# Sigmoids computed from tanh of half the argument in a two-layer hybrid trunk on one core

## The chip, the core and the metric

The kernel runs on one core of one Trainium2 chip. The metric is the device time of one execution in microseconds (us). Three runs of the kernel before took 2874.05, 2875.11 and 2875.87 us; the median is 2875.11 us.

## What is computed

The reference is one step of a trunk of two layers. The same weights serve 128 context tokens and 512 latent tokens, so 640 tokens run through everything. Each layer is a feed-forward sublayer, a mixer and another feed-forward sublayer, each with a layer norm. The mixer of the even layer joins windowed attention with a bidirectional mLSTM, that of the odd layer joins attention with a bidirectional HGRN2. Sigmoids stand in both mixers, and silu(x) is x * sigmoid(x):

```python
# even mixer, behind the two mLSTM scans
yb = sigmoid(bo) * rms(hf + flip(hb), norm_g)
# odd mixer
q = silu(cq)
def hgrn_gates(fp):
    f = lbh + (1.0 - lbh) * sigmoid(fp)
    return log(f), 1.0 - f
...
yc = rms(of + flip(ob), norm_g) * silu(cg)
```

The even mixer also needs log_sigmoid of its gates (computed with Abs, Exp and Ln), both need Exp for the softmax of the attention, and the feed-forward sublayers use silu.

## The kernel before, in words

All activations lie transposed, features on the 128 partitions and the 640 tokens along the free dimension, in two halves of 384 and 256 tokens (`HALVES`), or in five chunks of 128. Products with weights are done three times on split halves of the operands (`mm3`, `proj_pair`), so the weights are loaded with a DMA (`unit`), rounded on ACT and subtracted on DVE (`split`).

The mixers `even` and `odd` are written as Python generators, which `weave` runs in turn: one step of the attention, one step of the projections of the heads, and later steps of the mLSTM or HGRN2 heads. So instructions of the projections stand between those of the attention. The code is not the order on the engines: each engine runs a queue in order, and a planner sets these queues from the dependencies, the order of the code and its own view of the times.

The steps that matter here:

- `att_probs`: for one chunk of 128 queries and four heads, PE writes the scores into a bank (tile `s`), DVE takes the maximum, ACT takes Exp with a bias column and a sum (tiles `pq`, `E`, `bm`), DVE takes the reciprocal of the sum (`su`) and scales. `att_out` transposes the result on PE (`pT`), splits it on ACT and DVE (`pr`) and multiplies with the values (`pv`).
- `mlstm_in` (L1014), four heads: two projections with `proj_steps`, then `proj_pair` with five chunks. Of each chunk ACT copies the values (tile `va` or part of `mi`) and takes Sigmoid of the output gate `so`.
- `hgrn_cols` and `hgrn_in` (L1245, L1262), four heads: the projections for the query (Sigmoid, then a product on DVE) and for the two forget gates (Sigmoid, then multiply and add with the lower bound on DVE), each in two halves; then `proj_pair` with five chunks, of which ACT copies the values and takes Sigmoid of the gate, which DVE multiplies.
- `head_out` (L775): sum of squares on ACT, the power -1/2 on POOL (`hrs`), the product with the gate on DVE (`yn`), transposes on PE (`ho`), and a scale by the norm weight on ACT.
- `lower_bound` (L1229): a softmax over the two layers on [128, 8] numbers, on DVE and ACT.

ACT holds a table for the function that it evaluates. Where a function needs another one, the profile shows ACT_TABLE_LOAD as an instruction of ACT. Copy, Identity, Square and Abs show none in front of them.

Of the kernel before, what the change touches and what calls it, by code (L numbers as in the profile page):

```python
# [12 lines left out]
AF = mybir.ActivationFunctionType  # L13
ALU = mybir.AluOpType
# [3 lines left out]
P = 128  # L18
# [31 lines left out]
class Net:  # L50
# [721 lines left out]
            self.att_out(g, j, tiles, probs, vv, pr, yds[g])  # L772


    def head_out(self, hs, gate, g, yt, hf):  # L775

        nc = self.nc
        ch = CHUNKS[hf]
        a, b = HALVES[hf]
        k = len(ch)  # L780
        ss = self.sm(4, "ss")
        for n, c in enumerate(ch):
            self.act(self.ft(P, "junk"), hs[c], AF.Square, accum_out=ss[:, n:n + 1])
        self.ts(ss[:, :k], ss[:, :k], 1.0 / 128.0, ALU.mult, 1e-6, ALU.add)
        rs = self.sm(4, "hrs")
        nc.gpsimd.tensor_tensor(out=rs[:, :k], in0=ss[:, :k], in1=self.mhalf[:, :k], op=ALU.pow)
        ps = self.pm("ho")
        for n, c in enumerate(ch):
            yn = self.ft(P, "yn")
            self.stt(yn, hs[c], rs[:, n:n + 1], gate[:, c], ALU.mult, ALU.mult)  # L790
            self.tr(ps[:, n * P:(n + 1) * P], yn)
        y = self.ft(b - a, "yh")
        self.act(y, ps[:, :b - a], scale=g)
        self.split(yt[0][:, a:b], yt[1][:, a:b], y)
# [219 lines left out]
    def mlstm_in(self, ar, cols, w, h, heads):  # L1014

        nc = self.nc
        qT, kT = ar[0:2]
        so, va = (t.rearrange("p (c t) -> p c t", c=5) for t in ar[2:4])
        for col in cols:
            yield from self.proj_steps(w, *col)  # L1020

        def ev(t, p):
            self.act(va[:, t, 0:P], p[:, 0])
            self.act(so[:, t], p[:, 1], AF.Sigmoid)
        nc.gpsimd.memset(va[:, :, P:P + 1], 1.0)
        heads.append((qT, kT, va, so))
        yield from self.proj_pair(w, 1792 + h * P, 2320 + h * P, ev)

    def mlstm_head(self, h, ins, temps, yb, in_v, ma, col, tri, nident):

# [197 lines left out]

    def lower_bound(self):  # L1229

        nc = self.nc
        e = self.sm(8, "lbe").rearrange("p (l h) -> p l h", l=2)
        lg = self.v("c_lb", 0, 8).rearrange("p (l h) -> p l h", l=2)
        m = self.sm(4, "lbm")
        self.tt(m, lg[:, 0], lg[:, 1], ALU.max)
        self.tt(e, lg, m[:, None, :].to_broadcast([P, 2, 4]), ALU.subtract)
        self.act(e, e, AF.Exp)
        lb = self.sm(8, "lb").rearrange("p (l h) -> p l h", l=2)
        self.tt(m, e[:, 0], e[:, 1], ALU.add)
        nc.vector.reciprocal(out=m, in_=m)  # L1240
        self.tt(lb[:, 0], e[:, 1], m, ALU.mult)
        self.ts(lb[:, 1], lb[:, 0], -1.0, ALU.mult, 1.0, ALU.add)
        return lb

    def hgrn_cols(self, room, h, lb):  # L1245

        qT, f0, f1 = room[0:3]

        def evq(hf, p):
            a, b = HALVES[hf]  # L1250
            self.act(qT[:, a:b], p, AF.Sigmoid)
            self.tt(qT[:, a:b], qT[:, a:b], p, ALU.mult)

        def evf(f):
            def ev(hf, p):
                a, b = HALVES[hf]
                self.act(f[:, a:b], p, AF.Sigmoid)
                self.ts(f[:, a:b], f[:, a:b], lb[:, 1, h:h + 1], ALU.mult, lb[:, 0, h:h + 1], ALU.add)
            return ev
        return [(h * P, evq), (512 + h * P, evf(f1)), (1024 + h * P, evf(f0))]  # L1260

    def hgrn_in(self, room, cols, w, h, heads):  # L1262

        qT, f0, f1 = room[0:3]
        v, gt = (r.rearrange("p (c t) -> p c t", c=5) for r in room[3:5])
        for n, col in enumerate(cols):
            yield from self.proj_steps(w, *col, "v" if h == 0 and n < 2 else None)

        def evv(t, p):
            self.act(v[:, t], p[:, 0])  # L1270
            self.act(gt[:, t], p[:, 1], AF.Sigmoid)
            self.tt(gt[:, t], gt[:, t], p[:, 1], ALU.mult)
        heads.append((qT, (f0, f1), v, gt))
        yield from self.proj_pair(w, 1536 + h * P, 2048 + h * P, evv)

    def hgrn_head(self, h, ins, temps, yc, lmask, in_v):

        nc, i = self.nc, self.i
        qT, ft, v, gt = ins
# [16 lines left out]
        for lev in range(7):  # L1296
# [14 lines left out]
            else:  # L1311
                if lev == 5:
                    full = [self.bank(t, "full")[:, :b - a].rearrange("p (c t) -> p c t", t=P) for t, (a, b) in zip(("a2", "b"), HALVES)]
                    for hf, ch in enumerate(CHUNKS):
                        for r in range(4):
                            c = slice(32 * r, 32 * r + 32)
# [52 lines left out]
        o = [self.ft(b - a, "o") for a, b in HALVES]  # L1369
        for hf, ch in enumerate(CHUNKS):  # L1370
            ps = self.bank("b", "ov")
            for n, c in enumerate(ch):
                cc = slice(c * P, (c + 1) * P)
                out = ps[:, n * P:(n + 1) * P]
# [5 lines left out]
        o = [o[0][:, n * P:(n + 1) * P] for n in range(3)] + [o[1][:, n * P:(n + 1) * P] for n in range(2)]  # L1380
        yield
        yc.append(self.pair("yc", in_v))
        yt = yc[-1]
        for hf in range(2):
            self.head_out(o, gt, self.v("c_norm_g", h, 1), yt, hf)


    def run(self, upto=6):
# [95 lines left out]
```

## Time and profile before

| | us |
|---|---|
| median of three runs | 2875.11 |
| profiled execution, own time | 2878.58 |
| span from its first to its last instruction | 2876.8 |
| PE busy | 2718.5 |
| ACT busy | 1031.2 |
| DVE busy | 1824.1 |
| POOL busy | 346.8 |

PE is TensorE, ACT ScalarE, DVE VectorE, POOL GpSimd. A row of the timeline gives the start, the duration, the engine, the line, the operation, output and input tiles, the count, and in brackets the idle time of the engine ahead of it and what ended that. Every activation has line L123 and every matmul L136, since helpers record them; so the rows are told apart by their tiles. The mixer of the even layer lies between about 560 and 920 us, that of the odd layer between about 1920 and 2380 us; the rest is feed-forward.

### The profile page before, as it was taken

How to read it: one execution, taken by the hardware profiler on the slowest of the kernel's cores; microseconds unless marked ns; L12 is line 12 of the kernel's file. 1: busy time of each engine (PE TensorE's matmuls, PEld its weight loads, DVE VectorE, ACT ScalarE, POOL GpSimd, SP SyncE). 2: the span in 40 equal slices, each digit the busy share in tenths (PEclk: the TensorE clock that was granted, in tenths of full speed). 3: DMA queues.
4: the chain of work that ended last, by engine and by line, in shares of the span. 5: the costliest groups of instructions: out<-in, count | busy, mean ns of one | idle time of the engine just before them, and what ended most of it. 6: DMA issues, size and time to landing. Idle time of an engine off the chain costs nothing. (4 is left out here: it accounts for less than half of the span.)

```text
span 2876.8 us, 47326 instructions
## 1 busy us (share of the span) xinstructions
PE 2718.5 (94%) x19221; PEld 2608.6 (91%) x19221; DVE 1824.1 (63%) x3568; ACT 1031.2 (36%) x2063; POOL 346.8 (12%) x390
## 2 busy tenths in 40 slices
PE   6999999988998999999999999998999699999998
PEld 5999999977878999999999999987778589999997
DVE  8876865676557976533796673475567769333334
ACT  5421221566543511311422122156574435122122
POOL 4000000410002200000400000140104413000003
PEclk7999999999999999999999999999899799999999
DMA  7554543121222444422264452130111223223110
GB/s 198 179 147 125 168 118 92 60 62 39 61 67 70 147 147 125 125 72 68 59 184 132 125 154 86 40 99 16 37 38 55 76 72 119 80 74 96 59 52 37
DMA packets 321526, 270.56 MB, mean 94 GB/s; under 512 B 13834, under 2 KB 273692, under 8 KB 321308
## 3 DMA queue, kind: packets, MB, share of 16 engines
q1 hardware_dynamic: 320948, 267.39, 31.6%
q8 instruction: 151, 2.47, 0.4%
q14 instruction: 67, 0.55, 0.1%
q10 hardware_dynamic: 360, 0.14, 0.0%
HBM read 258.31 MB, written 9.18 MB: 93 GB/s over the span
## 5 line engine op out<-in xcount | busy, mean ns | idle before, releaser
L136 PE MATMUL ps<-h,w 128*128 128x256 f32 (+1 forms) x7584 | 1121.5, 309 | 1.8 <-DVE h L126 1.5
L136 PEld LDWEIGHTS ps<-h,w 128*128 128x128 f32 x7584 | 1114.8, 190 | 3.1 <-DVE h L126 2.1
L136 PE MATMUL po<-g,wv 128*128 128x256 f32 (+1 forms) x4224 | 631.9, 310 | 5.8 <-DVE x L133 5.8
L136 PEld LDWEIGHTS po<-g,wv 128*128 128x128 f32 x4224 | 622.7, 188 | 12.0 <-DVE x L133 6.9
L133 DVE SCALAR_TENSOR_TENSOR x<-po,mod,x 128x128 f32<-128x128 f32 (+1 forms) x576 | 235.8, 435 | 275.7 <-PE po L136 274.4
L133 DVE SCALAR_TENSOR_TENSOR acc<-rawa,sc,acc 128x512 f32<-128x512 f32 (+1 forms) x496 | 350.8, 746 | 14.0 <-DMA rawa<-in_ada_w 12.4
L126 DVE TENSOR_TENSOR w<-raw,w 128x1024 fp32r<-128x1024 f32 x212 | 262.3, 1243 | 128.0 <-ACT w L123 127.4
L123 ACT ACTIVATE wv<-raw 128x1024 fp32r<-128x1024 f32 x116 | 120.2, 1056 | 560.3 <-PE po L136 452.1
L123 ACT ACTIVATE w<-raw 128x1024 fp32r<-128x1024 f32 x212 | 222.2, 1056 | 168.3 <-issue 80.6
L463 POOL TENSOR_TENSOR ssq<-ssq,sq 128x384 f32<-128x384 f32 (+1 forms) x84 | 84.1, 1001 | 1337.3 <-ACT sq L123 1316.0
L123 ACT ACTIVATE g<-gt 128x384 fp32r<-128x384 f32 (+1 forms) x176 | 82.1, 467 | 403.0 <-DVE gt L126 402.7
L126 DVE TENSOR_TENSOR gt<-sl,ps 128x384 f32<-128x384 f32 (+1 forms) x176 | 85.4, 485 | 185.1 <-PE ps L136 180.4
L126 DVE TENSOR_TENSOR wv<-raw,wv 128x1024 fp32r<-128x1024 f32 x116 | 143.0, 1239 | 91.5 <-ACT wv L123 91.4
L136 PE MATMUL pj<-h,w 128*128 128x256 f32 (+1 forms) x1056 | 188.2, 321 | 0.4 <-DVE hi L126 0.4
L136 PEld LDWEIGHTS pj<-h,w 128*128 128x128 f32 x1056 | 164.0, 194 | 7.4 <-issue 3.9
L123 ACT ACTIVATE sl<-ps 128x384 f32<-128x384 f32 (+1 forms) x176 | 76.0, 433 | 232.6 <-PE ps L136 232.5
L136 PE MATMUL ps<-h,wv 128*128 128x256 f32 (+1 forms) x864 | 139.5, 314 | 2.9 <-ACT h L123 1.8
L136 PE MATMUL pn<-w,h 128*128 128x256 f32 x960 | 136.3, 289 | 0.7 <-DVE oc L126 0.7
L136 PEld LDWEIGHTS ps<-h,wv 128*128 128x128 f32 x864 | 129.3, 192 | 4.4 <-ACT h L123 2.1
L136 PEld LDWEIGHTS pn<-w,h 128*128 128x128 f32 x960 | 126.0, 194 | 2.6 <-DVE oc L126 1.1
L126 DVE TENSOR_TENSOR g<-gt,g 128x384 fp32r<-128x384 f32 (+1 forms) x176 | 85.7, 487 | 27.5 <-ACT g L123 27.5
L424 POOL TENSOR_SCALAR x<-x,agb 128x384 f32<-128x384 f32 (+1 forms) x80 | 74.1, 929 | 108.0 <-ACT h L123 72.6
(342 smaller groups left out, 2749.7 us busy)
## 6 DMA issues: line engine op xcount, KB each, us to landing
raw<-in_ffn_w SPq DMA_DIRECT2D x264, 512.0 KB
rawa<-in_ada_w SPq DMA_DIRECT2D x144, 512.0 KB
raw<-in_w_in_odd SPq DMA_DIRECT2D x18, 512.0 KB
raw<-in_w_in_even SPq DMA_DIRECT2D x14, 512.0 KB
raw<-in_w_in_even SPq DMA_DIRECT2D x16, 256.0 KB
raw<-in_w_out_even SPq DMA_DIRECT2D x8, 512.0 KB
raw<-in_w_in_odd SPq DMA_DIRECT2D x16, 256.0 KB
raw<-in_w_out_odd SPq DMA_DIRECT2D x8, 512.0 KB
```

Of the source, the lines that this page charges most:

```text
L123: return self.nc.scalar.activation(out=out, in_=in_, func=func, **k)
L126: return self.nc.vector.tensor_tensor(out=out, in0=in0, in1=in1, op=op)
L133: return self.nc.vector.scalar_tensor_tensor(out=out, in0=in0, scalar=s, in1=in1, op0=op0, op1=op1)
L136: return self.nc.tensor.matmul(out=out, lhsT=lhsT, rhs=rhs, start=start, stop=stop)
L424: nc.gpsimd.tensor_scalar(out=x, in0=x, scalar1=agb[:, 0, k:k + 1], scalar2=agb[:, 1, k:k + 1], op0=ALU.mult, op1=ALU.add)
L463: nc.gpsimd.tensor_tensor(out=sums[1], in0=sums[1], in1=sq, op=ALU.add)
```

## The change

Since sigmoid(x) = (1 + tanh(x/2)) / 2, ACT computes Tanh with scale 0.5 in place of Sigmoid, in all 64 places, and the rest of the formula goes elsewhere.

- Even mixer: after the five chunks of a head, one POOL operation on [128, 640] makes 0.5 * t + 0.5 of the gate.
- Odd mixer, query and gate: the product x * sigmoid(x) becomes (t + 1) * x, one scalar_tensor_tensor in place of a tensor_tensor, which is twice the value. The factor 2 of the query makes the head's output twice as large; `head_out` squares with scale 0.5, and the norm weight is multiplied by 0.25 for both factors.
- Odd mixer, forget gates: the lower bounds are changed from (lb, 1 - lb) to (0.5 + 0.5 lb, 0.5 - 0.5 lb), so the instruction behind Tanh stays as it was.

```diff
-    def head_out(self, hs, gate, g, yt, hf):
+    def head_out(self, hs, gate, g, yt, hf, scale=1.0):
...
-            self.act(self.ft(P, "junk"), hs[c], AF.Square, accum_out=ss[:, n:n + 1])
+            self.act(self.ft(P, "junk"), hs[c], AF.Square, scale=scale, accum_out=ss[:, n:n + 1])
...
         def ev(t, p):
             self.act(va[:, t, 0:P], p[:, 0])
-            self.act(so[:, t], p[:, 1], AF.Sigmoid)
+            self.act(so[:, t], p[:, 1], AF.Tanh, scale=0.5)
...
         yield from self.proj_pair(w, 1792 + h * P, 2320 + h * P, ev)
+        nc.gpsimd.tensor_scalar(out=ar[2], in0=ar[2], scalar1=0.5, scalar2=0.5, op0=ALU.mult, op1=ALU.add)
...
-        self.tt(lb[:, 0], e[:, 1], m, ALU.mult)
-        self.ts(lb[:, 1], lb[:, 0], -1.0, ALU.mult, 1.0, ALU.add)
+        self.tt(m, e[:, 1], m, ALU.mult)
+        self.ts(lb[:, 0], m, 0.5, ALU.mult, 0.5, ALU.add)
+        self.ts(lb[:, 1], m, -0.5, ALU.mult, 0.5, ALU.add)
...
-            self.act(qT[:, a:b], p, AF.Sigmoid)
-            self.tt(qT[:, a:b], qT[:, a:b], p, ALU.mult)
+            self.act(qT[:, a:b], p, AF.Tanh, scale=0.5)
+            self.stt(qT[:, a:b], qT[:, a:b], 1.0, p, ALU.add, ALU.mult)
...
-                self.act(f[:, a:b], p, AF.Sigmoid)
+                self.act(f[:, a:b], p, AF.Tanh, scale=0.5)
...
-            self.act(gt[:, t], p[:, 1], AF.Sigmoid)
-            self.tt(gt[:, t], gt[:, t], p[:, 1], ALU.mult)
+            self.act(gt[:, t], p[:, 1], AF.Tanh, scale=0.5)
+            self.stt(gt[:, t], gt[:, t], 1.0, p[:, 1], ALU.add, ALU.mult)
...
+        g = self.sm(1, "hg")
+        self.ts(g, self.v("c_norm_g", h, 1), 0.25, ALU.mult)
         for hf in range(2):
-            self.head_out(o, gt, self.v("c_norm_g", h, 1), yt, hf)
+            self.head_out(o, gt, g, yt, hf, 0.5)
```

## Rows read from the trace of the kernel before

**Rows 1.** The page, busy time, share and instructions of each engine.

```profile
PE 2718.5 (94%) x19221; PEld 2608.6 (91%) x19221; DVE 1824.1 (63%) x3568; ACT 1031.2 (36%) x2063; POOL 346.8 (12%) x390
```

**Rows 2.** Windows: stretch, length, busy PE, PEld, DVE, ACT, POOL; clock, DMA.

```profile
600.00:760.00 160.00, 142.57 (x928) 126.88 (x929) 106.21 (x271) 109.23 (x243) 10.70 (x15) 0.95 0.18 48
1960.00:2168.00 208.00, 187.42 (x1125) 154.81 (x1124) 128.84 (x333) 142.94 (x312) 14.65 (x17) 0.94 0.12 36
2500.00:2600.00 100.00, 100.00 (x686) 100.00 (x685) 36.34 (x58) 22.71 (x34) 0.00 (x0) 1.00 0.25 75
```

**Rows 3.** Groups, ACT, 500 to 1000 and 1900 to 2400: busy, mean ns.

```profile
L123 ACT ACT_TABLE_LOAD x26 | 33.4, 1283 | 0.3
...
L123 ACT ACT_TABLE_LOAD x34 | 43.6, 1283 | 2.4 <-issue 1.9
```

**Rows 4.** Timeline of ACT, 570 to 616 us.

```profile
576.35 1.28 ACT L123 ACT_TABLE_LOAD   x1
...
605.08 1.28 ACT L123 ACT_TABLE_LOAD   x1
...
612.48 1.28 ACT L123 ACT_TABLE_LOAD   x1
613.77 0.28 ACT L123 ACTIVATE mi<-pn 128x128 f32<-128x128 f32 x1
614.07 1.28 ACT L123 ACT_TABLE_LOAD   x1
```

**Rows 5.** Timeline of PE, both attention stretches; idle before, releaser in brackets.

```profile
617.53 0.79 PE L136 MATMUL s<-att 128*128 128x384 f32 x4 [0.39 <-ACT bm L123]
...
711.32 0.73 PE L136 MATMUL s<-att 128*128 128x512 f32 x2 [2.19 <-ACT pq L123]
713.79 1.08 PE L139 MATMUL pT<-ident,E 128*128 128x128 f32 x4 [1.74 <-DVE E L130]
...
2008.63 0.62 PE L136 MATMUL s<-att 128*128 128x384 f32 x2 [2.09 <-ACT pq L123]
...
2012.05 1.87 PE L139 MATMUL pT<-ident,pq 128*128 128x128 f32 x6 [1.39 <-DVE pq L130]
...
2126.23 0.62 PE L136 MATMUL s<-att 128*128 128x384 f32 x2 [2.08 <-ACT pq L123]
...
2146.52 1.66 PE L136 MATMUL pj<-h,w 128*128 128x384 f32 x8 [0.40 <-DVE hi L126]
```

**Rows 6.** Windows around the three longest of these waits.

```profile
708.00:722.00 14.00, 10.07 (x48) 8.02 (x46) 8.58 (x22) 9.71 (x18) 0.00 (x0) 0.76 0.27 73
...
2004.00:2022.00 18.00, 14.01 (x71) 10.56 (x70) 11.43 (x28) 11.82 (x26) 0.00 (x0) 0.81 0.20 58
...
2120.00:2134.00 14.00, 10.03 (x56) 8.01 (x56) 9.75 (x29) 12.29 (x29) 0.00 (x0) 0.88 0.01 4
```

**Rows 7.** Chain of waits in order of time: start, duration, engine, tile, line.

```profile
2000.63 1.28 ACT L123
...
2145.41 1.28 ACT L123
```

**Rows 8.** Groups of DVE, POOL and ACT by form.

```profile
L126 DVE TENSOR_TENSOR hi<-hi,pj 128x384 f32<-128x384 f32 x4 | 2.2, 550 | 1.7 <-ACT hi L123 1.7
...
L133 DVE SCALAR_TENSOR_TENSOR kT<-kT,oc,qrb 128x384 f32<-128x384 f32 x1 | 0.6, 612 | 0.4 <-PE qrb L136 0.4
...
L1284 POOL TENSOR_SCALAR harena<-hi 128x640 f32<-128x640 f32 x4 | 4.3, 1112 | 1.4 <-PE pn L136 1.4
...
L123 ACT ACTIVATE pq<-s,nm 128x384 f32<-128x384 f32 x40 | 23.2, 580 | 2.6 <-DVE nm L133 1.5 <-DVE nm L130 0.9
...
L123 ACT ACTIVATE hi<-pj 128x384 f32<-128x384 f32 x12 | 5.9, 489 | 9.5 <-PE pj L136 9.4
```

**Rows 9.** Timeline of POOL, head outputs of the even layer.

```profile
829.34 0.70 POOL L786 TENSOR_TENSOR hrs<-ss,mhalf 128x2 f32<-128x2 f32 x1 [5.68 <-DVE ss L130]
```

**Rows 10.** Timeline of ACT, first feed-forward sublayer.

```profile
94.51 0.21 ACT L123 ACTIVATE lbe<-lbe 128x8 f32<-128x8 f32 x1
```

## The prediction

> **What bounds the kernel now.** I read the engine shares first: PE is busy 94% of the span, ACT 36% [rows 1]. Then stretches, to see whether that holds everywhere. In a feed-forward stretch PE has no idle time at all (100.00 of 100 us), so nothing done for ACT can shorten it; in the two attention stretches, which are the ones that hold the sigmoids, PE works 142.57 of 160 and 187.42 of 208 us, at a mean granted clock of 0.95 and 0.94 [rows 2]. So 17.4 + 20.6 = 38.0 us of idle PE, and some time at the lower clock, is all that these stretches could give. Third, the groups of ACT by form: 26 table loads between 500 and 1000 us and 34 between 1900 and 2400 us, 1283 ns each, 77 us in all [rows 3]. Fourth, the timeline of ACT, to see what calls for them: a load stands ahead of a sigmoid and another ahead of the next softmax Exp, over and over, because the projections with the sigmoids are woven between the steps of the attention [rows 4]. Last, the idle times of PE and what ended them [rows 5], the clock around the largest [rows 6] and the chain of waits [rows 7]: these say which of the loads are waited for.
>
> **What goes.** In the even layer, 22 of the 26 loads alternate between Exp and Sigmoid (the other four: Exp, Ln and Exp of the gate rows, and Silu when the feed-forward begins). In the odd layer 32 of 34 do; the first load there has to stay in some form, since Silu was active before, and the last is for Silu. If Tanh and Exp are served by one table, 54 loads go: 54 x 1.283 = 69.3 us of ACT's 1031.2 [rows 1, 3]. That is no saving in time by itself, ACT being idle most of the span; I count only where PE stood still behind a load.
>
> **Three large places.** (A) At 711.32 us PE had waited 2.19 us for the exponentials of one head, behind which its score bank is freed; two loads lie in the microseconds before. Then 1.74 us for probabilities scaled on DVE [rows 5]. The first goes whole, as the two loads are 2.57 us. Of the second I let 0.7 go: the chain sum, reciprocal, scaling on DVE follows the last Exp and remains. After these waits the granted clock fell to 0.5 (the 1.2 GHz level): 0.76 over 14 us is 14 x 0.24 / 0.5 = 6.7 us at the lower level [rows 6], some 5.4 of it with PE at work, which costs half, 2.7 us. Sum 2.2 + 0.7 + 2.7 = 5.6 us. (B) At 2008.63 PE waited 2.09 us in the same way, 0.40 for the next pair, and 1.39 at the transposes [rows 5]; with 0.4 of the last going that is 2.9. The clock, 0.81 over 18 us [rows 6], means 6.8 us at the lower level, some 4.4 of them at work: 2.2 us. Sum 5.1. (C) The same pattern at 2126.23, with 2.08 [rows 5] and waits of 0.40 and 1.39 behind it; clock 0.88 over 14 us is 3.4 us at the lower level, 2.4 at work, 1.2 us [rows 6]. Sum 4.1.
>
> **Small places.** Five shorter waits of PE stand behind a load, from the 0.39 us at 617.53 to the 0.40 us at 2146.52 [rows 5], two in the even layer and three in the odd one: some 2.4 us, all taken. Total: 5.6 + 5.1 + 4.1 + 2.4 = 17.2 us.
>
> **A second count.** The chain of waits covers the odd layer. Ten table loads stand on it as ACT pieces without a tile, the first at 2000.63 and the last at 2145.41 [rows 7]: 12.8 us. My odd-layer terms (B, C and 1.6 of the small ones) are 10.8. The chain does not cover the even layer, where I have 6.4; with these the second count is 19.2. I take 18, between 17.2 and 19.2.
>
> **Bounds.** Below: only the direct waits for exponentials go, 2.2 + 2.1 + 2.1 = 6.4, with the small ones 7. Above: every wait in A, B and C (3.9 each), their clock (6.1) and all small gaps with an Exp or a scaling at their end (6) make 24; the 38 us of idle time contain waits that have nothing to do with tables, and I don't reach for them. What is gained is not given back later: behind each mixer lies a stretch in which PE is never idle [rows 2].
>
> **What is added.** The Tanh activations have the shapes of the 64 Sigmoids and a constant scale. The rows show no Tanh. The nearest are the Sigmoid itself, 489 ns on 128x384 from PSUM, and the Exp of that shape, 580 ns with a bias column and a sum beside it [rows 8]. I take 489, so no change; at the dear end 64 x 0.09 = 5.8 us of ACT come back against 69 that go, hidden by ACT's idle time. That a Tanh is cheaper could only add to ACT's idle time. 28 products (8 for q, 20 for the gate) turn from tensor_tensor into scalar_tensor_tensor: 128x384 from PSUM takes 550 ns in the first form and 612 in the second [rows 8], so at most 28 x 0.062 = 1.7 us of DVE, in the stretch where DVE works 128.84 of 208 us [rows 2]; hidden, and 1.7 us if not. The four scaled norm weights and one more operation in the lower bounds are five DVE operations on 1 to 4 columns, whose inputs are there from the start; at worst some 1 us. Each even head adds one POOL operation on 128x640, 1.11 us by its nearest row [rows 8]; POOL is busy 10.70 of 160 us there [rows 2]. It waits for the head's last gate and whatever POOL does next is queued behind it. For heads 0 to 2 that is tens of microseconds later. For head 3 it is the power at 829.34 [rows 9], on which the transposes of the head output wait; if POOL has the new operation first, up to 1.2 us are lost there. I take 0 for all additions; 1.7 + 1.2 + 1 make 4 us the bad end.
>
> **A rule against the rows, twice.** The rows: a load takes 1.28 us and the next activation starts 0.01 us behind it (612.48, 613.77 [rows 4]), with no other gap. The Trainium skill (ScalarE: Activation LUTs, What ACT_TABLE_LOAD costs) adds a drain of about 1.38 us to each load, about 2.66 us per switch. By that the ten loads on the chain would be worth 26.6 us instead of 12.8, and the total some 32. The trace shows no room for it, so 1.28 stays. The other place concerns which functions share a table, and it is the first rival.
>
> The rows show a load at 576.35 ahead of the Ln of the gate rows, after an Exp, and one at 605.08 ahead of the next Exp [rows 4]: there Exp and Ln alternate as Sigmoid and Exp do, and each is loaded apart. The Trainium skill (ScalarE: Activation LUTs, Table sets: the hidden batching unit) puts Exp and Tanh into one set, and Exp and Ln into another that holds both. The first would confirm the forecast; in the second the trace doesn't follow the page.
>
> **Rivals.**
> 1. The loads stay, because Tanh is given a table of its own. For: Exp and Ln don't share here [rows 4], and no row shows Tanh. Against: nothing in the trace. Then ACT has the same loads at the same places, and the additions cost 0 to 4 us: 2875 to 2879, say 2877. Chance 0.10.
> 2. The loads go, and PE meets the next wait. The scaling on DVE, the bank of the transposes and PE's fixed order stay, and only the direct waits are won: 7 us less, 2868. For: the waits of 1.39 and 1.74 us on DVE stand right behind those on ACT [rows 5]. Against: PE had projections to run in these same steps, and the clock fell only where both came together [rows 6]. Chance 0.16.
> 3. Slower: the order on the engines changes. The order is not the code's: the Exp of the lower bounds, written at the start of the odd layer, ran at 94.51 us [rows 10], so a planner sets it from its own view of times. With 28 changed and a few new operations it may put score matmuls of a head ahead of the projections that cover the softmax. One such place costs what A, B and C do, about 5 us each. Three or four new ones eat the gain; from five on it is slower, 2875 - 18 + 25 = 2882. Against: ACT's, PE's and nearly all of DVE's instructions are the same in number and shape. Chance 0.06.
>
> **How the numbers follow.** The profiled execution took 2878.58 us (span 2876.8), 3.5 above the median 2875.11, or 0.12%; the savings are differences inside it and are taken off the median: 2875.1 - 18 = 2857. Forecast 0.68, the rivals 0.10, 0.16 and 0.06. Under the forecast the time lies between 2851 (24 less) and 2866 (half of the 18); rival 2 with the additions, 7 - 4 = 3 less, carries the upper end to 2872. Below, I add 5 us for waits that I could not ascribe: 2846. No change is within 0.2%, 5.75 us, about what a measurement can tell. Faster by more than that: the forecast and two thirds of rival 2, 0.79 in all; within it rival 1 and the rest of rival 2, 0.15; slower rival 3, 0.06.
>
> **What would show it.** Right: nine or ten table loads instead of 63; no idle time of PE of about 2 us that ends with an Exp around A, B and C; granted clock 1.00 there; ACT's busy time lower by some 69 us. Step by step: if the loads are gone and PE still waits about 4 us at those places, the terms A to C were DVE's; if PE waits are gone but the clock isn't 1.00, the clock terms are wrong. Wrong: loads at their old number, or new waits of PE of several microseconds elsewhere in the attention stretches.

## The result and the profile after

The changed kernel takes 2853.2 us, the median of four runs (2846.81, 2852.66, 2853.76, 2854.92), against 2874.6 for the kernel before (2874.05 to 2875.87): 21.4 us less, ratio 0.9916 with a 95% interval of 0.9903 to 0.9928. A later comparison gave 0.9894 (0.9875 to 0.9912). The forecast was 2857, 18 us less.

The profiled execution took 2846.81 us, span 2845.0, and is the fastest of the four; it is 31.8 us shorter than the profiled execution of before, where the medians differ by 21.4. The page's row of engines, against [rows 1]:

```profile
PE 2703.4 (95%) x19221; PEld 2597.6 (91%) x19221; DVE 1819.8 (64%) x3573; ACT 961.4 (34%) x2009; POOL 353.8 (12%) x394
```

The table loads in the groups of ACT over the whole span, against [rows 3]:

```profile
L123 ACT ACT_TABLE_LOAD x9 | 11.5, 1283 | 9.1 <-DMA vstage<-in_ln_b 7.7 <-issue 1.2
```

63 loads have become 9, and ACT is busy 69.8 us less, where 69.3 were forecast. Windows of the same lengths as in [rows 6], around the same score products, places A, B and C (columns as in [rows 2]). The order has changed, so they do not hold the same instructions otherwise:

```profile
696.00:710.00 14.00, 13.90 (x102) 12.65 (x100) 10.44 (x28) 8.69 (x24) 0.74 (x1) 1.00 0.03 5
1980.00:1998.00 18.00, 17.44 (x108) 14.25 (x107) 13.30 (x35) 11.17 (x31) 0.00 (x0) 1.00 0.11 33
2092.00:2106.00 14.00, 13.90 (x90) 12.07 (x89) 11.04 (x30) 8.90 (x27) 0.32 (x1) 1.00 0.16 44
```

At all three PE now works nearly without a gap, and the granted clock is 1.00 where it was 0.76, 0.81 and 0.88. The waits of 2.19, 2.09 and 2.08 us [rows 5] are gone; at B 0.22 us is left.

For the comparisons below I use two stretches that hold the same work in every kernel: the even one from the first transpose of the mixer to the first transposed head output, the odd one from the first `qrt` to the first `lv`. First the kernel before, then the changed one:

```profile
581.51:816.25 234.74, 214.35 (x1419) 191.17 (x1417) 152.59 (x405) 143.51 (x339) 16.72 (x25) 0.96 0.19 53
1906.81:2185.18 278.37, 252.37 (x1569) 214.03 (x1566) 167.13 (x433) 176.43 (x401) 39.46 (x44) 0.95 0.12 35
```

```profile
580.77:807.37 226.60, 209.91 (x1418) 188.16 (x1417) 153.04 (x405) 116.05 (x318) 19.98 (x28) 0.98 0.19 55
1892.37:2152.35 259.98, 246.47 (x1569) 212.37 (x1566) 163.33 (x433) 136.12 (x369) 40.77 (x44) 0.97 0.13 37
```

The even stretch is 8.1 us shorter and the odd one 18.4, together 26.5. PE's own time for the same instructions fell too, by 4.4 and 5.9 us, as the mean granted clock rose from 0.96 to 0.98 and from 0.95 to 0.97. What lies outside the two stretches is no guide: among the nine profiles of the table further down it takes between 2357 and 2371 us, in no order that follows the change.

### The profile page after: what moved, and what is told of

Same layout as the page of the kernel before. It is cut to its first block, busy times and chain, and to the rows that moved or that the text cites. A ratio compares the mean times of both kernels' runs of the same rounds, so it can differ in the third digit from the quotient of the medians.

```text
span 2845.0 us, 47283 instructions
## 1 busy us (share of the span) xinstructions
PE 2703.4 (95%) x19221; PEld 2597.6 (91%) x19221; DVE 1819.8 (64%) x3573; ACT 961.4 (34%) x2009; POOL 353.8 (12%) x394
## 3 DMA queue, kind: packets, MB, share of 16 engines
q8 instruction: 151, 2.47, 0.4%
## 4 chain that ended last, share of the span: by engine, by line
PE 73%; DVE 13%; DMA 5%; ACT 3%; issue 3%; POOL 2%; SPq 0%; DVEq 0%; ACTq 0%; POOLq 0%
PE ps L136 35%; PE po L136 21%; PE pj L136 5%; PE pn L136 3%; DVE acc L133 3%; DMA rawa<-in_ada_w 2%; DMA raw<-in_ffn_w 2%; PE pv L136 2%; DVE w L126 2%; PE pT L139 1%; PE s L136 1%; DVE wv L126 1%; DVE x L133 1%; DVE h L126 1%; DVE sum L126 1%
## 5 line engine op out<-in xcount | busy, mean ns | idle before, releaser
L133 DVE SCALAR_TENSOR_TENSOR acc<-rawa,sc,acc 128x512 f32<-128x512 f32 (+1 forms) x496 | 351.2, 747 | 12.9 <-DMA rawa<-in_ada_w 11.5
```

The costliest lines, as they stand in the source:

```text
L133: return self.nc.vector.scalar_tensor_tensor(out=out, in0=in0, scalar=s, in1=in1, op0=op0, op1=op1)
```

## The experiments

### Part by part: does the gain come with the loads, and do the parts add up?

Number one: Tanh without any of the additions (and the same edit at the three other places).

```
-            self.act(so[:, t], p[:, 1], AF.Sigmoid)
+            self.act(so[:, t], p[:, 1], AF.Tanh)
```

> The kernel before with Tanh written for Sigmoid in all four places and nothing else: no scale of 0.5, no products with the added 1, no scaled bounds, norm weights or output, so what it computes in the two gates, the queries and the forget gates is another function. All 54 table loads between Exp and Sigmoid go, none of the additions comes. Theory 1 (the gain is PE's waits behind ACT, freed by the loads; additions cost nothing): the same time as the changed kernel, 2853 within 2 us, ACT busy about 70 us below before. Theory 2 (much of the gain is the new order that the planner chose in the changed kernel): this kernel gets a third order, and its time differs from 2853 by more than 4 us to either side. Theory 3 (the loads are worth more, and the additions give some of it back): 1 to 4 us faster than the changed kernel, 2849 to 2852.

Measured: ratio 0.9917 (0.9903 to 0.9931), 9 loads.

Number two: all the additions, with the loads.

```
-            self.act(so[:, t], p[:, 1], AF.Tanh, scale=0.5)
+            self.act(so[:, t], p[:, 1], AF.Sigmoid, scale=0.5)
```

> The changed kernel with Sigmoid for Tanh, all else as in it: the scale of 0.5, the fused products, the POOL operation, the scaled bounds and weights are there, so the gates are computed as another function, and all 63 loads are there. Theory 1: the additions cost nothing, 2875 within 2 us. Theory 2 (order): anything that differs from 2875 by more than 4 us, to either side, with the loads at their old number. Theory 3: slower than before by what the additions cost, 2876 to 2879.

Measured: ratio 1.000 (0.9987 to 1.0012), 63 loads. So the additions cost nothing that can be measured, from either side, and without Tanh nothing is gained.

Numbers three and four: the change in one layer alone.

```
 even only:  so by Tanh with scale=0.5, and the tensor_scalar on POOL; all of the odd layer as before
 odd only:   qT, f, gt by Tanh with scale=0.5, stt for tt, scaled bounds and norm weights; the even layer as before
```

> The change in the even layer alone (the output gate by Tanh, and the POOL operation), the odd layer as before: 22 loads go, 32 stay. The prediction's term is 6.4 us, by which 2868.7. By the landmarks of the two profiled executions the even layer gave some 12 us, by which 2863. Theory 2: the even layer takes a third course, with waits of PE in other places, and the two halves do not add up to the whole 21.4 us.

> The change in the odd layer alone (queries, forget gates and output gate by Tanh, fused products, scaled bounds and norm weights), the even layer as before: 32 loads go, 22 stay. The prediction's term is 10.8 to 12.8 us, by which 2862 to 2864. By the landmarks of the profiled executions the odd layer gave up to 18 us, of a profiled execution that is 7 us below the median: 2857 to 2862. Theory 1: this gain and that of the even layer alone add up to 21.4 within 2 us. Theory 2: they do not.

Measured: even 0.9976 (0.9966 to 0.9986), 41 loads; odd 0.9926 (0.9914 to 0.9938), 31 loads. On the 2879.2 us of before in that comparison these are 6.9 and 21.3 us. The even part is what the prediction said (6.4). The odd part is 1.7 to 2 times its term (10.8 to 12.8). The sum, 28 with some 4 either way, agrees with the whole (21 to 28 us by the interval of the first comparison, 25 to 36 by that of the later one).

### The loads or the order?

The lists of instructions in the traces show that the planner gave the changed kernel another order on PE, DVE and ACT; that of POOL differs by the four added operations alone. Where a doubled term comes from can't be told while both change at once. So the two were parted: the kernel is planned with one function, and on the finished lists the other is put in its place before the loads are placed.

Number five: the order of before and what each instruction waits for, without the loads. Number six: those of the changed kernel, with the loads.

```
+    swap(nc, AF.Sigmoid, AF.Tanh)      # five, in the kernel before; six: swap(nc, AF.Tanh, AF.Sigmoid) in the changed one
+def swap(nc, frm, to):
+    ...
+            block.instructions = [replace(i, func=to) if type(i).__name__ == "InstActivation" and i.func == frm else i
+                                  for i in block.instructions]
```

> The kernel before, planned with Sigmoid, and Tanh put in its place afterwards on the finished instruction lists: every engine keeps the order and the waits of before, only the 54 table loads are gone (what the gates compute is another function). Theory 1 (the gain is the loads' own time, behind which PE waits): ratio to before 0.991 to 0.993, as for Tanh with a plan of its own (0.9917), and the waits of PE for score banks and transposes in the odd attention fall from 5.5 and 6.4 us to below 1 each. Theory 2 (the planner's new order earns a good part): the direct waits alone, 7 to 12 us, ratio 0.996 to 0.9975, and the waits at the transposes stay.

> The changed kernel, planned with Tanh, and Sigmoid put in its place afterwards on the finished instruction lists: the order and the additions of the changed kernel, with the 54 loads back (the gates compute another function). Theory 1: no gain is left, ratio 1.000 to 1.003, the upper end if an order made for an ACT without loads stands them worse than one made with them. Theory 2: the order carries a good part of the gain by itself, ratio 0.995 to 0.997.

Measured: five 0.9947 (0.9928 to 0.9966), six 1.0075 (1.0057 to 1.0093). Neither theory holds as it stood. Taking away the loads alone gives half of the gain or less; the new order alone is no gain but a loss of 21.6 us, as long as the loads are there. In the same comparison the changed kernel ran once more:

> The changed kernel once more, beside the others on the same chip. The first four runs were 2846.81 and 2852.66 to 2854.92 us, and the even part alone and the odd part alone gave 7 and 21 us, 28 together, against 21.4 for the whole. If the parts add up and the first comparison was low, the ratio to before is 0.990; if something is given back when both are there, 0.9915 to 0.992. In its trace the waits of PE in the two attention stretches should be those of the first profile, 15.3 and 12.8 us.

Measured: 0.9894 (0.9875 to 0.9912), 2852.43 us against 2866.95 for number five and 2902.59 for number six. That is the side on which the parts add up. PE's waits in its trace are 15.7 and 12.9 us.

Number five's profiled execution was the longest of its seven. So it was repeated (ten), and beside it the changed kernel was given an order made for Sigmoid in the same way (nine: number two, with the swap of number five).

> The changed kernel with all its additions, but planned with Sigmoid in the place of Tanh, and Tanh put in afterwards on the finished instruction lists: it computes what the changed kernel computes, with an order made for 63 loads. Theory 1, restated after the fifth run (the loads' own time gives the direct waits for score banks and some clock; the rest, the waits at the transposes, goes only with the planner's new order): ratio 0.994 to 0.9955, 13 to 17 us; in the trace PE's waits for score banks (s) in the two attention stretches fall from 8.5 to about 2.5 us, those at the transposes (pT) stay at 9 to 10.5. Rival (the fifth run's median or its profile was off, and the order is worth little): 0.9895 to 0.992, and pT waits about 2.

> The kernel of the fifth run once more, whose profiled execution was 14 us longer than the median of its other six (2881.12 against 2862 to 2869). The order of before with Tanh on the finished lists. If the fifth run's ratio holds: 0.9935 to 0.9955. If the profiled execution was the typical one: 0.998 to 1.000. PE's waits in the two attention stretches as in the fifth run's trace, 17.6 and 21.5 us within 1, whatever the time; the mean granted clock in the odd one 0.95 to 0.96 where it was 0.93.

Measured: nine 0.9966 (0.9953 to 0.9978), ten 0.9974 (0.9960 to 0.9987). So three measurements of the old order without loads, in two comparisons, give 15.3, 9.8 and 7.5 us: the loads are worth about 10 us in that order, less than I expected for nine and ten, and the odd clock in ten was 0.94, not 0.95 to 0.96. The waits came out about as expected: those for score banks fall from 8.5 to 2.9 us in nine, those at the transposes stay at 9.4, and ten's sums are 16.9 and 20.3 us, the second 0.2 below its range. First PE's waits in the odd stretch of the kernel before, by tile, line and releaser: us in total, times, longest.

```profile
PE qrt L139 <- POOL qrp L1159: 9.5, 8, 1.7
PE pT L139 <- DVE pq L130: 6.4, 16, 1.4
PE s L136 <- ACT pq L123: 5.5, 5, 2.1
PE pv L136 <- DVE pr L126: 1.9, 4, 1.1
```

The same view of number nine (old order, no loads):

```profile
PE qrt L139 <- POOL qrp L1161: 9.5, 8, 1.7
PE pT L139 <- DVE pq L130: 5.6, 14, 1.4
PE s L136 <- ACT pq L123: 2.2, 4, 0.7
PE pv L136 <- DVE pr L126: 1.9, 4, 1.0
```

Of number six (new order, with the loads):

```profile
PE s L136 <- ACT pq L123: 15.4, 11, 2.5
PE qrt L139 <- POOL qrp L1161: 8.3, 8, 1.3
...
PE pT L139 <- DVE pq L130: 1.2, 3, 0.6
```

And of the changed kernel (new order, no loads):

```profile
PE qrt L139 <- POOL qrp L1161: 8.5, 8, 1.4
PE pv L136 <- DVE pr L126: 0.9, 2, 0.6
...
PE s L136 <- ACT pq L123: 0.8, 3, 0.3
...
PE pT L139 <- DVE pq L130: 0.6, 1, 0.6
```

Read the rows of `s` and `pT` across the four. Taking the loads away shortens the waits for the exponentials (`s`), from 5.5 to 2.2. It leaves those at the transposes (`pT`), which wait for DVE. The new order takes those away, from 5.6 to 0.6, whether the loads are there or not (1.2); but with the loads it pays 15.4 for the exponentials. That holds for the odd stretch. In the even one the new order with the loads lengthens the waits at the transposes too, so there the order helps only without them. The row of `pT` in the even stretch, for before, nine, six and the changed kernel:

```profile
PE pT L139 <- DVE E L130: 4.0, 5, 1.7
...
PE pT L139 <- DVE E L130: 3.8, 4, 1.7
...
PE pT L139 <- DVE E L130: 10.2, 7, 2.8
...
PE pT L139 <- DVE E L130: 1.5, 3, 0.9
```

What the order does is seen at place C. PE's timeline in number nine:

```profile
2117.23 0.52 PE L136 MATMUL pn<-w,h 128*128 128x256 f32 x3
2118.45 0.62 PE L136 MATMUL s<-att 128*128 128x384 f32 x2 [0.70 <-ACT pq L123]
2119.47 0.62 PE L136 MATMUL s<-att 128*128 128x384 f32 x2 [0.40 <-ACT pq L123]
2121.47 1.87 PE L139 MATMUL pT<-ident,pq 128*128 128x128 f32 x6 [1.39 <-DVE pq L130]
```

And in the changed kernel:

```profile
2095.55 0.62 PE L136 MATMUL s<-att 128*128 128x384 f32 x2
2096.02 2.31 PE L136 MATMUL pn<-w,h 128*128 128x256 f32 x18
2098.17 0.52 PE L136 MATMUL pj<-h,w 128*128 128x384 f32 x2
2098.60 0.62 PE L136 MATMUL s<-att 128*128 128x384 f32 x2
2099.30 1.67 PE L136 MATMUL pj<-h,w 128*128 128x384 f32 x8
2100.80 0.38 PE L139 MATMUL pT<-ident,pq 128*128 128x128 f32 x2
2100.94 0.60 PE L136 MATMUL pj<-h,w 128*128 128x384 f32 x2
```

In the old order the two last score products and the first transposes stand one behind the other, with no projection between them, and PE waits three times. In the new one 20 projection matmuls stand between the scores, 8 ahead of the first transpose and 2 between each pair of transposes. They cover the chain of Exp, reciprocal and scaling, which has not become shorter: from the end of the last Exp to the first transpose 1.7 us pass in number nine and 1.9 in the changed kernel. Number one has the same order at this place with nothing changed but the function, so nothing in the dependencies forbade it before; the planner chose it only where it planned with Tanh. Why it did so was not looked into.

By the lists of instructions in the traces, two, five, nine and ten have the order of before up to some 20 of PE's 19221 instructions, and one, six and seven that of the changed kernel; between the two orders some 700 stand at another place. The two stretches in nine profiles, summed (PE's waits are the sums of the rows of the view used above, for both stretches):

| order planned with | loads | kernels | length, us | PE's waits, us | PE busy, us | granted clock, odd stretch |
|---|---|---|---|---|---|---|
| Sigmoid | 63 | before, two | 513.1, 517.5 | 45.7, 44.6 | 466.7, 472.2 | 0.95, 0.93 |
| Sigmoid | 9 | five, nine, ten | 507.9, 507.8, 504.9 | 39.1, 38.2, 37.2 | 468.0, 467.9, 466.1 | 0.93, 0.93, 0.94 |
| Tanh | 9 | after, seven, one | 486.6, 490.7, 489.8 | 28.1, 28.6, 28.2 | 456.4, 460.5, 459.4 | 0.97, 0.96, 0.96 |
| Tanh | 63 | six | 541.0 | 59.8 | 479.1 | 0.93 |

Between the means of the first two lines lie 8.4 us: 7.0 of waits and 2.1 of PE's own time, less 0.7 that these columns don't show. Between the second and third lie 17.9: 9.9 of waits and 8.6 of PE's own time, less 0.6. The 2.1 us are less than the spread within a line (up to 5.5 us of PE's own time), so that the loads alone give anything by the clock is not shown. By layers, the loads give 5.3 us of the even stretch and 3.1 of the odd one (where executions of one line differ by up to 4.1), the order 2.6 and 15.3. By the timings, it is 7.5 to 15.3 us for the loads, and 14.5 for the order in the comparison that held both (2866.95 to 2852.43). These shares hold for this sequence, first the loads and then the order; in the new order the same 54 loads cost 50 us (2902.59 against 2852.43).

### One load more taken off PE's path

Number eight: one more Exp, behind the Ln of the gate rows, in the changed kernel.

```
         self.act(u, u, AF.Ln)
+        self.act(self.sm(1, "pre")[0:64], u[:, 0:1], AF.Exp)
```

> The changed kernel with one more Exp of a 64x1 column straight behind the Ln of the gate rows. Its table load then falls into time in which ACT is idle, and the load at 604.33 us, behind which PE waits 7.93 us for the gate rows, is no longer there. Theory 1 (a load costs its 1.28 us only where PE waits behind it): that wait falls from 7.9 to 6.6 us, the number of loads stays 9, and the time falls by 1.3 us, or some 2 us if the granted clock recovers too: less than the timing can tell, ratio to the changed kernel 0.999 to 1.000. Rival: the planner's order changes elsewhere by as much, and the time differs by more than 3 us to either side.

Measured: 2850.64 us, 0.9899 (0.9880 to 0.9917), beside 2852.43 for the changed kernel: no difference that can be measured, as expected. The load itself behaves as Theory 1 says. ACT, where the load now stands, and PE's wait for the gate rows:

```profile
579.65 1.28 ACT L123 ACT_TABLE_LOAD   x1
580.94 0.20 ACT L123 ACTIVATE pre<-rows 64x1 f32<-64x1 f32 x1
```

```profile
607.12 1.33 PE L139 MATMUL pm<-ident,rows 128*128 128x128 f32 x5 [6.65 <-ACT rows L123]
```

7.93 us have become 6.65: here a load on PE's path costs its 1.28 us, and one beside it nothing that can be measured.

## Why the prediction was right, and where its reasons were not

- **Which loads go** was right to the number: 54, and ACT's busy time with them.
- **No drain behind a load**: the switch was taken at 1.28 us, and number eight, which moved one load off the path, shortened PE's wait by 1.28. The Trainium skill (ScalarE: Activation LUTs, What ACT_TABLE_LOAD costs) gives about 2.66 us for a switch, with a drain; the traces agree with the load that it states and do not show the drain.
- **Direct waits of A, B and C** (6.4 us): in the old order without loads they fall by 2.2, 1.4 and 1.4. 0.7 stays at B and C, and goes only with the new order.
- **The second waits** (0.7 of 1.74 at A, 0.4 behind B and 0.4 behind C): this step failed in its mechanism. Without the loads and in the old order they are 1.74, 1.39 and 1.39, as before, since DVE's chain and the 0.40 in front of it at B and C are the same. Place A in number nine:

```profile
712.74 0.74 PE L139 MATMUL pT<-ident,E 128*128 128x128 f32 x4 [1.74 <-DVE E L130]
```

  Yet all of it goes in the changed kernel, and the smaller ones of its kind too (10.4 us of `pT` in both stretches, 2.1 after), by the new order.
- **The clock** (6.1 us): too small. PE's own time in the two stretches falls by 10.7 us between the means of the first and third lines of the table, and 8.6 of that comes with the order, as the clock in the odd stretch rises from 0.93 to 0.96 only there. I had counted the low clock around three waits alone.
- **Small places** (2.4 us, all taken): of the two that the prediction names, the 0.39 us at 617.53 goes with the loads. The 0.40 us at 2146.52 stays in number nine and goes only with the new order, so it was no cost of a load:

```profile
2139.72 1.66 PE L136 MATMUL pj<-h,w 128*128 128x384 f32 x8 [0.40 <-DVE hi L133]
```

- **Even 6.4, odd 10.8 to 12.8**: the even part was measured at 6.9, the odd at 21.3. The odd term is the one that was mis-sized: the loads that it counts give 3.1 us of that stretch in the profiles, and the order, which it has at nothing, 15.3. Nor did the ten loads on the chain of waits (12.8 us, the second count) come back as time while the order stayed.
- **Additions at 0**: right (ratio 1.000 with the loads; 0.9917 without them against 0.9916 with them and the additions). The Tanh on 128x384 takes 486 ns, the Sigmoid took 489 [rows 8]. The products take 554 ns on 128x384 in the new form, and 554 in the old form in number one. The POOL operation takes 0.78 us on average, less than the 1.11 of its nearest row, and for the last head the power is queued behind it as was feared:

```profile
819.50 0.73 POOL L1029 TENSOR_SCALAR mi<-mi 128x640 f32<-128x640 f32 x1 [4.71 <-ACT mi L123]
820.19 0.70 POOL L786 TENSOR_TENSOR hrs<-ss,mhalf 128x2 f32<-128x2 f32 x1
```

  PE's wait there is nevertheless 0.25 us, and 0.56 at the products ahead of it, where it was 2.47. By the releasers of the profile the 2.47 are due not to POOL but to a DMA that writes a state out, for which ACT waits ahead of the last sum of squares. ACT's row in the kernel before and in the changed one:

```profile
828.66 0.31 ACT L123 ACTIVATE junk<-mi 128x128 f32<-128x128 f32 x1 [2.27 <-DMA out_new_state_b_n<-C]
...
818.68 0.31 ACT L123 ACTIVATE junk<-mi 128x128 f32<-128x128 f32 x1 [1.16 <-DMA out_new_state_b_n<-C]
```

  It differs from one execution to the next: numbers five and ten are the same kernel, without the POOL operation, and PE waits 2.13 and 0.27 us there.
- **Rival 2** (7 us less, 2868, PE's fixed order stays) is what taking away the loads alone does: 8.4 us in the profiles, 7.0 of them waits, and 9.8 us by the timing of number nine. I gave it 0.16 because PE "had projections to run in these same steps". It had; but that they are run there is the planner's choice.
- **Rival 3** was right that the planner's order changes, and wrong in the sign. Its argument against, that the instructions are the same in number and shape, was no argument: the function alone changed the order. The loss it priced at 5 us a place does occur where order and loads don't fit: number six has eleven waits for `pq` of up to 2.5 us in the odd stretch, and is 21.6 us slower than before.

So the total of 18 came out near by luck, because two errors met: too much put down to the loads (17.2, against 8.4 in the profiles and 7.5 to 15.3 by the timings), and nothing to the order (14.5 by the timings, 17.9 in the profiles).

## What to carry to other kernels

Where a planner sets the order, an edit that changes the time an engine needs has two effects, the time itself and the order chosen for it. Count the first in the fixed order (here the waits for DVE behind the freed engine stayed whole), and allow a second term for the waits that other ready work could cover; here, in the profiles, it was twice the first. To part them, swap the function on the finished lists, both ways: here the order was worth more than the 54 loads, and was harmful without their removal.

## What the runs showed of the hardware that was not expected

Tanh runs without a load of its own behind Silu as well. ACT's timeline of the changed kernel at the beginning of the odd attention: the last load before it is that for the Silu of the feed-forward, at 930.31; three Tanh activations of the first head run, and the first load comes for the Exp behind them.

```profile
1907.85 0.46 ACT L123 ACTIVATE hi<-pj 128x384 f32<-128x384 f32 x1
...
1923.62 0.38 ACT L123 ACTIVATE hi<-pj 128x256 f32<-128x256 f32 x1 [2.59 <-PE pj L136]
...
1944.06 0.49 ACT L123 ACTIVATE hi<-pj 128x384 f32<-128x384 f32 x1 [1.85 <-PE pj L136]
...
1947.28 1.28 ACT L123 ACT_TABLE_LOAD   x1 [1.25 <-issue]
```

In the kernel before, the load stood in front of the first of these, at 1922.40. And the granted clock did not follow the waits in proportion here. In the odd stretch 24 to 26 us of PE's waits went with a granted clock of 0.93 to 0.95; taking 4 us off, as numbers five, nine and ten do, left it at 0.93 to 0.94; taking 12 off raised it to 0.96 to 0.97. Each of these is one execution.
